# A hybrid decoder layer on one core: turned query and key rows split over 128 partitions, and another order of the last products of the output projection

## The chip, the cores and the metric

The kernel runs on one core of a Trainium2 chip. The metric is the device time of one execution in microseconds (us), lower is better. The engines are TensorE (PE in the profile, its weight loads PEld), VectorE (DVE), ScalarE (ACT), GpSimd (POOL) and SyncE (SP), which issues nearly all DMAs. Each engine works through its own list in order; semaphores tie the lists together.

## The reference

One decoder layer over 1024 tokens of width 1024, all in float32. One normed input projection feeds two groups of heads; their outputs are joined, projected, added to the residual and passed through a squared-ReLU MLP.

```python
h = rms_norm(x, norm1_w[l])
proj = h @ w_in[l]
da_q = rms_norm(da_q.reshape(B, S, DA_HEADS, 2, DA_QK_DIM), q_norm_w[l])   # 4 heads, two 64-wide maps each
da_k = rms_norm(da_k.reshape(B, S, DA_HEADS, 2, DA_QK_DIM), k_norm_w[l])
da_o = diff_attention(da_q, da_k, da_v, lam)     # (softmax(q1 k1^T) - lam * softmax(q2 k2^T)) v, causal
...
dn_o = gated_delta_rule(dn_q, dn_k, dn_v, g, beta)      # 4 heads, 128 wide, chunks of 64
...
mix = jnp.concatenate([da_o.reshape(B, S, DA_WIDTH), dn_o.reshape(B, S, DN_WIDTH)], axis=-1)
x = x + mix @ w_out[l]
h = rms_norm(x, norm2_w[l])
x = x + jnp.square(jax.nn.relu(h @ w_up[l])) @ w_down[l]
```

## The kernel before

**Precision.** Products that need more than one pass of the array take each float32 operand as a rounded part (fp32r, names ending in H) and a remainder (names ending in L), and sum three matmuls: high by high, high by low, low by high. Lines 1012 to 1014, 1291 to 1293 and 1452 to 1454 are such triples, each matmul 128x128 by 128x512.

**Tokens** come in 8 blocks of 128 (NT = 8). `tiles` lists them from the last to the first, and the projection's position i means block `tiles[i]`.

**Stages.** Up to about 260 us come the input norm, the projections of the gated DeltaNet heads and the preparation of their chunks. From 260 to about 620 us several streams are woven together. After that the MLP runs as two Strassen-like series of products with nothing else beside it.

**The planner.** The woven stretch is written as Python generators: `scan` and `scan_out` (the DeltaNet recurrence), `da_units` (the projection for the differential attention), `da_turns` (transposes of its normed queries and keys), `scores` and `values` (softmax and its product with v), `mix_loads` and `mixed` (transposes of the heads' outputs), `outproj` (output projection and second norm), `backs` and `up_first` (transposes and the first products of the MLP). `Interleave` holds a clock, `flow.now`, that only TensorE's work advances (`flow.pe`); `flow.chain` books the costs of ACT and DVE steps and gives the time when a result should be there. At each step the generator of the lowest priority number that is due goes on. So TensorE's order is fixed by these estimates when the kernel is built; the other engines' instructions and the DMAs are ordered by the framework's own scheduling. A put-off store (`flow.put_off`) is issued when its planned time is reached, or before its buffer is taken again (`flow.begun`).

**Queries and keys.** `da_units` makes for each token block 512 projected columns; `leave` (from line 1027) copies them out on ACT (lines 1035 and 1040), norms them per 64 columns and hands tiles of 256 columns (two heads) to `late`. For each of 32 such tiles (two pairs of heads, query or key, 8 blocks) `da_turns` does two transposes (lines 965 and 966) into one bank of `px`, a PSUM pool with two banks that five other streams use too. The bank then holds 128 partitions, 64 for each of the two softmax maps of a head, by two heads of 128 tokens. For map m the rounded rows go to their own 64 partitions of `qa[:, m]` and the remainder to the other 64, so that one contraction over 128 partitions gives high by high plus low by low, and with the halves swapped (`qb`) the two cross terms. That is two ACT instructions (line 972) and two DVE ones (line 973) over 64 partitions each. One DMA (line 977) stores the 256 KB tile to `qk_d`; `qa` has two buffers. `load_head` (line 1068) reads the keys of a head back as `KS`, `load_q` (lines 1085 to 1087) the queries of a block as `qa` and `qb`, both in pieces of 512 bytes.

**Weights.** `load_unit` brings a unit's weights through two buffers `wraw` (line 211), rounds them on ACT (line 213) and takes the remainder on DVE (line 214). The last such units here are those of the output projection.

**Output projection.** `outproj` first adds the products of the DeltaNet half of `mix`. Then `todo` holds 16 products of the attention half, each 12 matmuls for one block and one half of the columns (n = 0 left, n = 1 right): all left ones first, then all right ones. It takes the first in the list whose block has landed; a right one needs its left one done, and either all scores done and i < 4, or `state["free"]`, which `mixed` sets after the last block has been turned. Each product is added to `accs` (line 1298). After the right one `norm2` stores the row of 1024 (line 1308, 512 KB), squares it on ACT (line 1310) and scales it on DVE (line 1316) into `hn`, a tile of the pool `ae` that has four buffers and otherwise holds the softmax tiles `pexp`. `backs` turns the normed blocks: those of i < 4 through `keep`, which takes a row tile of the eight that `accs` used (lines 250 to 257), the others through `turn_b` (line 1384). `feed` fills further row tiles with the first weights of the MLP (line 1430).

Of the kernel before, what the change touches and what calls it, by code (L numbers as in the profile page):

```python
# [9 lines left out]
F32 = mybir.dt.float32  # L10
F32R = mybir.dt.float32r
BF16 = mybir.dt.bfloat16
AF = mybir.ActivationFunctionType
ALU = mybir.AluOpType
# [4 lines left out]
P = 128  # L19
# [3 lines left out]
NT = SEQ // P  # L23
# [96 lines left out]
def act(n, accum=False):  # L120
    return "S", 55.0 + 0.83 * n + (93.0 if accum else 0.0)


def vec(n, extra=0.0):
    return "V", 68.0 + 1.045 * n + extra
# [7 lines left out]
def tile_hymba_layer(  # L133
# [6 lines left out]
    nc = tc.nc  # L140
    V, S, G, T = nc.vector, nc.scalar, nc.gpsimd, nc.tensor
# [9 lines left out]
    dram = ctx.enter_context(tc.tile_pool(name="dram", bufs=1, space=DRAM))  # L151
# [36 lines left out]
    fsg_d = dram.tile([P, 1024], F32, name="fsg_d")  # L188
    rt_d = dram.tile([SEQ], F32, name="rt_d")
    cgr_d = dram.tile([HEADS * SEQ], F32, name="cgr_d")  # L190
    qk_d = dram.tile([2, 2, NT, P, 2, 2, P], F32, name="qk_d")
    v_d = dram.tile([NT, P, 3, P], F32, name="v_d")
    acc_d = dram.tile([NT, P, DM], F32, name="acc_d")
    ud = {i: dram.tile([FF // 512, P, 2, 512], F32, name=f"ud{i}") for i in range(1, 8)}
# [261 lines left out]
    for tb in range(NT):  # L456
        T.matmul(tail[:, 300 + 2 * tb:302 + 2 * tb], ssum_[:, tb * P:(tb + 1) * P], ones[:, 0:2],
                 start=True, stop=True)
# [288 lines left out]
    ae = actx.enter_context(tc.tile_pool(name="ae", bufs=4, **right))  # L747
# [16 lines left out]
    flow = Interleave()  # L764
# [189 lines left out]

    late, accs, vts, v_at, qa_free = [], {}, {}, {}, [0.0] * 3

    def da_turns():
        for i in range(4 * NT):
            while not late:
                yield flow.now + 50, None  # L960
            g, kind, tb, qn, t = late[0]
            r = yield from flow.bank("px", at=max(t + 2000, qa_free[i % 2] - 500))
            late.pop(0)
            pt = px.tile([P, 512], F32, tag="px", name="ps_qkt")
            T.transpose(pt[:, 0:P], qn[:, 0:P], ident)
            T.transpose(pt[:, P:2 * P], qn[:, P:2 * P], ident)
            flow.begun(("qa", i % 2))
            qa = sd.tile([P, 2, 256], F32R, tag="qa", name="qa", bufs=2)
            wv = qw if kind == 0 else kw
            for m in range(2):  # L970
                a, b = HF[m], HF[1 - m]
                S.activation(qa[a, m, :], pt[a, 0:256], AF.Copy, scale=wv[a])
                V.scalar_tensor_tensor(qa[b, m, :], pt[a, 0:256], wv[a], qa[a, m, :].bitcast(F32),
                                       ALU.mult, ALU.subtract)
            flow.pe(2 * TR)
            t = flow.chain(act(256), act(256), vec(256, 60), vec(256, 60), start=max(flow.now, qa_free[i % 2]))
            flow.put_off(t, ("qa", i % 2), lambda g=g, kind=kind, tb=tb, qa=qa: nc.sync.dma_start(
                qk_d[g, kind, tb], qa.bitcast(F32).rearrange("p m (h t) -> p m h t", h=2)))
            qa_free[i % 2] = t + DMA_T
            flow.hold(r, t)  # L980
            state["turned"] += 1
            if state["turned"] % (2 * NT) == 0:
                flow.due(lambda t, key: key[0] == "qa")
                state["da"] += 1
                state["da_t"] = flow.now + 6000
        sdctx.close()
# [77 lines left out]
    def load_head(h, pool):  # L1064
        KS = []
        for m in range(2):
            k = pool.tile([P, SEQ], F32R, tag=f"KS{m}", name=f"KS{m}")
            nc.sync.dma_start(k.bitcast(F32).rearrange("p (b t) -> p b t", t=P),
                              qk_d[h // 2, 1, :, :, m, h % 2, :].rearrange("b p t -> p b t"))
            KS.append(k)  # L1070
        return KS

# [8 lines left out]
    def load_q(h, tb):  # L1081
        qa = ap.tile([P, 2, P], F32R, tag="qa", name="qa", bufs=2)
        qb = ap.tile([P, 2, P], F32R, tag="qb", name="qb", bufs=2)
        src = qk_d[h // 2, 0, tb, :, :, h % 2, :]
        nc.sync.dma_start(qa.bitcast(F32), src)
        nc.sync.dma_start(qb[HF[0]].bitcast(F32), src[HF[1]])
        nc.sync.dma_start(qb[HF[1]].bitcast(F32), src[HF[0]])
        return qa, qb

    order = [(0, t) for t in range(NT)] + [(1, t) for t in range(NT)]  # L1090
    order += [(h, t) for t in reversed(range(NT)) for h in (2, 3)]
    ready = []

    def scores():
        heads, loaded, npe, nsc, since = {}, {}, 0, 0, 0
# [5 lines left out]
        for u, (h, tb) in enumerate(order):  # L1101
# [29 lines left out]
            n = (tb + 1) * P  # L1131
            npc = 1 if n <= 512 else 2
            pl = n // npc
            pe, ssum = [], ap.tile([P, 2], F32, tag="ssum", name="ssum", bufs=4)
            mx = ap.tile([P, 2], F32, tag="mx", name="mx", bufs=4)
            for m in range(2):
                nsc += 1
                if state["scan"] and nsc % 2:
                    name, sc = "rsc", pools["rsc"]
                else:  # L1140
                    name, sc = "qsc", qsc
                yield 0, name
                sc = sc.tile([P, 1024], F32, tag="sc", name="ps_sc")
                for pc in range(npc):
                    o = sc[:, 512 * pc:512 * pc + pl]
                    ks = KS[m][:, pc * pl:(pc + 1) * pl]
                    last = pc == npc - 1
                    T.matmul(o, qa[:, m, :], ks, start=True, stop=False)
                    T.matmul(o, qb[:, m, :], ks, start=False, stop=not last)
                    if last:  # L1150
                        T.matmul(sc[:, 512 * pc + pl - P:512 * pc + pl], identr, caus, start=False, stop=True)  # L1151
                scv = sc.rearrange("p (a b) -> p a b", b=512)[:, :npc, :pl]
                V.tensor_reduce(mx[:, m:m + 1], scv, axis=AX.XY, op=ALU.max, negate=True)  # L1153
                npe += 1
                ep = pools["be"] if state["scan"] and npe % 3 == 0 else ae
                e = ep.tile([P, SEQ], F32, tag="pexp", name="pexp")
                S.activation(e[:, :n].rearrange("p (a b) -> p a b", a=npc), scv, AF.Exp, bias=mx[:, m:m + 1],  # L1157
                             accum_out=ssum[:, m:m + 1])
                flow.pe(2 * max(n / 2.4, 110.0) + 55)
                t = flow.chain(vec(n), act(n, True))  # L1160
                flow.hold(name, t)
                pe.append(e)
# [4 lines left out]
            V.scalar_tensor_tensor(pe[0][:, :n], pe[1][:, :n], cf, pe[0][:, :n], ALU.mult, ALU.add)  # L1167
            t = flow.chain(vec(10), vec(1, 60), vec(n, 100), start=t - flow.HOP)
            q = load_q(*order[u + 1]) if u + 1 < len(order) and order[u + 1][0] // 2 < state["da"] else None
            ready.append((h, tb, pe[0], ri, vt, t))  # L1170
        state["scored"] = True

    turn_no = [0]
# [1 line left out]
    def values():  # L1175
        for _ in order:
            while not ready or ready[0][5] > flow.now:
                yield (flow.now + 100 if not ready else ready[0][5]), None
            h, tb, pe, ri, vt, _t = ready[0]
            while v_at.get(tb, 1e12) > flow.now:  # L1180
                yield flow.now + 50, None
            vt = vt or vts[0]
# [96 lines left out]
    def outproj():  # L1279
# [23 lines left out]
        def norm2(tb, pos):  # L1303
            w2b = pools["w2b"] if state["free"] else w2b0
            hn = ae.tile([P, SEQ], F32, tag="pexp", name="hn2")
            hn = [hn[:, 0:512], hn[:, 512:1024]]
            ss = laid("nss")
            nc.sync.dma_start(acc_d[tb], accs[tb])
            for i in range(2):
                S.activation(hn[i], accs[tb][:, 512 * i:512 * i + 512], AF.Square, accum_out=ss[:, i:i + 1])  # L1310
            V.tensor_tensor(ss[:, 0:1], ss[:, 0:1], ss[:, 1:2], ALU.add)
            r = laid("nr")
            rstd(r, ss[:, 0:1], 1.0 / DM, EPS, None, "nrt", 1)
            for i in range(2):
                sl = slice(512 * i, 512 * i + 512)
                normed_by[:] = [V.scalar_tensor_tensor(hn[i], accs[tb][:, sl], r, w2b[:, sl], ALU.mult, ALU.mult)]
            t = flow.chain(act(512, True), act(512, True), vec(1), vec(1), ("G", 1800.0))
            return hn, flow.chain(vec(512, 60), vec(512, 60), start=t - flow.HOP)
# [17 lines left out]
        aw = dctx.enter_context(tc.tile_pool(name="aw", bufs=1, **right))  # L1336
        w2b0 = aw.tile([P, DM], F32, name="w2b0")
        nc.sync.dma_start(w2b0, norm2_w.partition_broadcast(P))
        todo = [(n, i) for n in range(2) for i in range(NT)]
        left0 = NT  # L1340
        flow.add(6, up_first())
        flow.add(4.5, backs())
        while todo:
            j = next((j for j, (n, i) in enumerate(todo) if landed.get((tiles[i], 0), 1e12) <= flow.now
                      and (n == 0 or (0, i) not in todo) and (n == 0 or state["scored"] and i < 4 or state["free"])), None)
            if j is None:
                yield flow.now + 50, None
                continue
            n, i = todo.pop(j)
            yield from half(0, (w0, w1)[n], n, tiles[i])  # L1350
            if n == 0:
                left0 -= 1
                if left0 == 0:
                    pools["wu"] = first_ops(0), unit_time("V", 610.0)
            else:
                hns[i] = norm2(tiles[i], i)
                normed2.add(i)
                feed()
# [496 lines left out]
```

## Time and profile before

| | us |
|---|---|
| time before, median of 3 runs (1225.75 to 1227.22) | 1226.64 |
| the profiled execution | 1226.58 |
| its span, first to last instruction | 1224.9 |
| ACT at line 972, 64 instructions | 29.26 |
| DVE at line 973, 64 instructions | 30.48 |
| TensorE's waits of 0.2 us and more, summed | 9.1 |

The stretches and their busy time tell where an engine sits idle; a wait is named by the line that waited and by what ended it. Matmuls overlap, so their durations add up to more than the time that they take, and the distance between two starts is what counts. The granted clock is 1.00 nearly everywhere.

### The profile page before, as it was taken

To read this page: it belongs to the slowest core of one execution; us is meant where nothing else is said; L and a number is where in the kernel's file an instruction comes from. 1 tells how busy PE (TensorE), PEld (TensorE's weight loads), DVE (VectorE), ACT (ScalarE), POOL (GpSimd) and SP (SyncE) were. 2 spreads that over 40 slices of the span, in tenths; PEclk is the share of its full clock that TensorE was granted. 3 is DMA by queue.
4 is the path that set the end of the run, shared out by engine and by line. 5 is a ranking of instruction groups with operands and counts; after the bars stand their busy time and mean duration, and the time that the engine had idled before them with its cause. 6 is when DMAs were issued, how large, how long until landed. Compare 5 with 4: busy or idle time off the path is not lost.

```text
span 1224.9 us, 17632 instructions
## 1 busy us (share of the span) xinstructions
PE 1212.0 (99%) x6330; PEld 1029.2 (84%) x6330; DVE 850.0 (69%) x1448; ACT 604.6 (49%) x1176; POOL 121.0 (10%) x162
## 2 busy tenths in 40 slices
PE   9999999999999999999999999999999999999998
PEld 9988888898888888888788888888888888888887
DVE  7786788477868577766798554566577955786553
ACT  8565545234556555656666444454554333333331
POOL 0011110223332230212100000000000000000000
PEclk9999999999999999999999999999999999999999
DMA  6564442456755584434528433443279855433301
GB/s 230 176 182 125 112 130 87 116 183 218 241 161 180 173 244 135 115 80 142 183 86 291 155 127 133 170 174 135 103 253 353 325 185 183 160 104 104 138 35 69
DMA packets 161087, 199.04 MB, mean 163 GB/s; under 512 B 21008, under 2 KB 120936, under 8 KB 161000
## 3 DMA queue, kind: packets, MB, share of 16 engines
q1 hardware_dynamic: 160856, 197.79, 49.3%
q8 instruction: 50, 0.82, 0.3%
q14 instruction: 37, 0.30, 0.1%
q10 hardware_dynamic: 144, 0.13, 0.0%
HBM read 132.32 MB, written 65.56 MB: 162 GB/s over the span
## 4 chain that ended last, share of the span: by engine, by line
PE 89%; DVE 4%; DMA 3%; ACT 2%; issue 1%; SPq 0%; POOL 0%; ACTq 0%; DVEq 0%
PE X L1454 5%; PE X L1453 5%; PE X L1452 5%; PE X L1768 4%; PE X L1769 4%; PE X L1770 4%; PE ps_dn L221 4%; PE ps_dn L219 4%; PE ps_dn L220 4%; PE ps_qk L1012 3%; PE Y L1454 3%; PE Y L1453 3%; PE Y L1452 3%; PE ps_qk L1014 3%; PE ps_qk L1013 2%; PE ps_o L1201 2%
## 5 line engine op out<-in xcount | busy, mean ns | idle before, releaser
L1371 ACT CAST hH<-ur 128x1024 fp32r<-128x1024 f32 x56 | 58.6, 1048 | 166.0 <-PE X L1769 79.7
L1372 DVE TENSOR_TENSOR hL<-ur,hH 128x1024 fp32r<-128x1024 f32 x56 | 68.5, 1224 | 79.8 <-ACT hH L1371 79.8
L1372 DVE TENSOR_TENSOR op<-raw,op 128x1024 fp32r<-128x1024 f32 x48 | 58.7, 1223 | 75.3 <-PE X L1453 42.3
L1768 PE MATMUL X<-hH 128*128 128x512 f32 x224 | 87.2, 389 | 0.0
L1769 PE MATMUL X<-hL,hH 128*128 128x512 f32 x224 | 87.2, 389 | 0.0
L1770 PE MATMUL X<-hH,hL 128*128 128x512 f32 x224 | 87.2, 389 | 0.0
L1012 PE MATMUL ps_qk<-wH,hH 128*128 128x512 f32 x192 | 82.2, 428 | 1.9 <-ACT qn L1040 1.9
L1014 PE MATMUL ps_qk<-wH,hL 128*128 128x512 f32 x192 | 75.8, 395 | 0.0
L219 PE MATMUL ps_dn<-hH,wH 128*128 128x512 f32 x192 | 75.7, 394 | 0.0
L220 PE MATMUL ps_dn<-hL,wH 128*128 128x512 f32 x192 | 75.6, 394 | 0.0
L1013 PE MATMUL ps_qk<-wL,hH 128*128 128x512 f32 x192 | 75.4, 393 | 0.1
L221 PE MATMUL ps_dn<-hH,wL 128*128 128x512 f32 x192 | 75.4, 393 | 0.0
L1372 DVE TENSOR_TENSOR hL<-dw,hH 128x1024 fp32r<-128x1024 f32 x56 | 68.2, 1220 | 3.2 <-ACT hH L1371 3.2
L1371 ACT CAST op<-raw 128x1024 fp32r<-128x1024 f32 x48 | 50.4, 1050 | 34.8 <-PE Y L1454 20.1
L1371 ACT CAST hH<-dw 128x1024 fp32r<-128x1024 f32 x56 | 58.6, 1047 | 16.7 <-DMA dw<-in_w_down_dram 5.1
L1157 ACT ACTIVATE pexp<-ps_sc,mx 128x128 f32<-128x128 f32 (+7 forms) x64 | 47.3, 740 | 26.1 <-DVE mx L1153 26.1
L595 DVE SCALAR_TENSOR_TENSOR cy<-cp,pv,cy 128x512 f32<-128x512 f32 x72 | 53.7, 750 | 7.8 <-ACT cy L593 7.0
L1153 DVE TENSOR_REDUCE mx<-ps_sc 128x1 f32<-128x128 f32 (+7 forms) x64 | 47.5, 754 | 14.1 <-PE ps_sc L1151 13.5
L1291 PE MATMUL ps_op<-wH,hH 128*128 128x512 f32 x128 | 53.6, 419 | 0.0
L1293 PE MATMUL ps_op<-wH,hL 128*128 128x512 f32 x128 | 50.3, 393 | 0.0
L1292 PE MATMUL ps_op<-wL,hH 128*128 128x512 f32 x128 | 50.0, 391 | 0.0
L1453 PE MATMUL Y<-hL,op 128*128 128x512 f32 x128 | 49.8, 389 | 0.0
(355 smaller groups left out, 3383.8 us busy)
## 6 DMA issues: line engine op xcount, KB each, us to landing
ur<-ud SPq DMA_DIRECT2D x28, 1024.0 KB, 4.9
raw<-in_w_up_dram SPq DMA_DIRECT2D x32, 512.0 KB, 3.7
dw<-in_w_down_dram SPq DMA_DIRECT2D x32, 512.0 KB, 7.2
qk_d<-qa SPq DMA_DIRECT2D x32, 256.0 KB, 3.1
ud<-ua SPq DMA_DIRECT2D x16, 512.0 KB, 4.0
ud<-s SPq DMA_DIRECT2D x16, 512.0 KB, 3.2
wraw<-in_w_in_dram SPq DMA_DIRECT2D x24, 256.0 KB, 3.5
wraw<-in_w_in_dram SPq DMA_DIRECT2D x48, 128.0 KB, 2.9
```

Source lines behind the costliest of these rows:

```text
L219: T.matmul(ps, lh(k), rh(k), start=(k == 0), stop=False)
L220: T.matmul(ps, lh(k), rl(k), start=False, stop=False)
L221: T.matmul(ps, ll(k), rh(k), start=False, stop=(k == n - 1))
L1012: T.matmul(ps, hH[:, 4 * kh + k, sl], wh[:, k, :], start=(kh + k == 0), stop=False)
L1013: T.matmul(ps, hH[:, 4 * kh + k, sl], wl[:, k, :], start=False, stop=False)
L1014: T.matmul(ps, hL[:, 4 * kh + k, sl], wh[:, k, :], start=False, stop=(kh + k == 4))
L1371: S.copy(dst[0], src)
L1372: V.tensor_tensor(dst[1], src, dst[0].bitcast(F32), ALU.subtract)
L1453: T.matmul(ps, op[0][:, k, cs], h[1][:, k, :], start=False, stop=False, skip_group_check=True)
L1768: T.matmul(o, v[0][:, j, sl], v[2][:, j, c], start=s0, stop=False, skip_group_check=True)
L1769: T.matmul(o, v[0][:, j, sl], v[3][:, j, c], start=False, stop=False, skip_group_check=True)
L1770: T.matmul(o, v[1][:, j, sl], v[2][:, j, c], start=False, stop=s1, skip_group_check=True)
```

## The change

The names of the diff are those of the section before. The turned tile is split once: ACT rounds all 128 partitions into `qa[:, 0]`, DVE writes the remainder of all 128 into `qa[:, 1]`. Since `qk_d` shall still hold, for each map, 64 high and 64 low rows (for the second map low first), its index is now map, row, head, token, and `store_halves` writes each tile with two DMAs of 128 KB: the rounded rows to the first and fourth block of 64 rows, the remainder to the second and third. The planner books one ACT and one DVE step instead of two and two. The loads read the same 512-byte pieces under the new index.

In `outproj`, `todo` lists left and right products of positions 0 to 3, then those of 4 to 7. `in_ae` counts the tiles taken from `ae`; each entry of `ready` carries the number of its first softmax tile, and before `free` a right product may only run if the next tile of `ae` doesn't take the place of one that an entry of `ready` still holds.

```diff
-    qk_d = dram.tile([2, 2, NT, P, 2, 2, P], F32, name="qk_d")
+    qk_d = dram.tile([2, 2, NT, 2, P, 2, P], F32, name="qk_d")
...
+    def store_halves(dst, qa):
+        blocks = dst.rearrange("m (j r) h t -> (m j) r (h t)", j=2)
+        for part, to in ((0, blocks[0:4:3]), (1, blocks[1:3])):
+            nc.sync.dma_start(to, qa[:, part, :].bitcast(F32))
...
-            for m in range(2):
-                a, b = HF[m], HF[1 - m]
-                S.activation(qa[a, m, :], pt[a, 0:256], AF.Copy, scale=wv[a])
-                V.scalar_tensor_tensor(qa[b, m, :], pt[a, 0:256], wv[a], qa[a, m, :].bitcast(F32),
-                                       ALU.mult, ALU.subtract)
+            S.activation(qa[:, 0, :], pt[:, 0:256], AF.Copy, scale=wv)
+            V.scalar_tensor_tensor(qa[:, 1, :], pt[:, 0:256], wv, qa[:, 0, :].bitcast(F32), ALU.mult, ALU.subtract)
             flow.pe(2 * TR)
-            t = flow.chain(act(256), act(256), vec(256, 60), vec(256, 60), start=max(flow.now, qa_free[i % 2]))
-            flow.put_off(t, ("qa", i % 2), lambda g=g, kind=kind, tb=tb, qa=qa: nc.sync.dma_start(
-                qk_d[g, kind, tb], qa.bitcast(F32).rearrange("p m (h t) -> p m h t", h=2)))
+            t = flow.chain(act(256), vec(256, 60), start=max(flow.now, qa_free[i % 2]))
+            flow.put_off(t, ("qa", i % 2), lambda g=g, kind=kind, tb=tb, qa=qa: store_halves(qk_d[g, kind, tb], qa))
...
-                              qk_d[h // 2, 1, :, :, m, h % 2, :].rearrange("b p t -> p b t"))
+                              qk_d[h // 2, 1, :, m, :, h % 2, :].rearrange("b p t -> p b t"))
...
-        src = qk_d[h // 2, 0, tb, :, :, h % 2, :]
+        src = qk_d[h // 2, 0, tb, :, :, h % 2, :].rearrange("m p t -> p m t")
...
+                mine.append(in_ae[0] if ep is ae else 1e9)
+                in_ae[0] += ep is ae
...
-            ready.append((h, tb, pe[0], ri, vt, t))
+            ready.append((h, tb, pe[0], ri, vt, t, mine[0]))
...
-        todo = [(n, i) for n in range(2) for i in range(NT)]
+        todo = [(n, i) for g in range(2) for n in range(2) for i in range(4 * g, 4 * g + 4)]
...
-                      and (n == 0 or (0, i) not in todo) and (n == 0 or state["scored"] and i < 4 or state["free"])), None)
+                      and (n == 0 or (0, i) not in todo) and (n == 0 or state["free"] or state["scored"] and i < 4 and all(in_ae[0] - 4 < x[6] for x in ready))), None)
```

More of the change, by code (lines that the diff above doesn't have):

```diff
@@ L1091, in tile_hymba_layer @@
     order += [(h, t) for t in reversed(range(NT)) for h in (2, 3)]
-    ready = []
+    ready, in_ae = [], [0]
     def scores():
@@ L1133, in scores @@
             pl = n // npc
+            mine = []
             pe, ssum = [], ap.tile([P, 2], F32, tag="ssum", name="ssum", bufs=4)
@@ L1178, in values @@
                 yield (flow.now + 100 if not ready else ready[0][5]), None
-            h, tb, pe, ri, vt, _t = ready[0]
+            h, tb, pe, ri, vt, _t, _ = ready[0]
             while v_at.get(tb, 1e12) > flow.now:
@@ L1305, in norm2 @@
             hn = ae.tile([P, SEQ], F32, tag="pexp", name="hn2")
+            in_ae[0] += 1
             hn = [hn[:, 0:512], hn[:, 512:1024]]
```

## The prediction

> **What bounds the kernel now.** I read the page's spans, then TensorE's waits, then busy time and granted clock by stretch, then the chain of waits behind the largest gap, then the DMA view of single stores.
>
> ```profile
> span 1224.9 us, 17632 instructions
> PE 1212.0 (99%) x6330; PEld 1029.2 (84%) x6330; DVE 850.0 (69%) x1448; ACT 604.6 (49%) x1176; POOL 121.0 (10%) x162
> ```
>
> TensorE is busy for 1212.0 of 1224.9 us. The change removes no matmul, so the question is what it does to the 12.9 us of gaps, to the clock, and whether it opens new gaps. Four rows of TensorE's timeline show that order alone costs nothing:
>
> ```profile
> 532.51 0.60 PE L1189 MATMUL ps_at<-ident,pexp 128*128 128x128 f32 x4
> 532.86 0.48 PE L1291 MATMUL ps_op<-wH,hH 128*128 128x512 f32 x1
> 533.18 0.40 PE L1292 MATMUL ps_op<-wL,hH 128*128 128x512 f32 x1
> 533.41 0.39 PE L1293 MATMUL ps_op<-wH,hL 128*128 128x512 f32 x1
> ```
>
> Starts count, not durations: in steady state a 512-column matmul follows every 0.23 us. Four small ones and the first large one take 0.67 us together, so a small one costs 0.11 us wherever it stands. A new order of the same matmuls moves the time only through waits.
>
> ```profile
> 258.00:620.00 362.00, 354.48 (x2065) 305.90 (x2066) 266.88 (x629) 208.55 (x544) 88.67 (x109) 1.00 0.57 174
> 306.40:308.80 2.40, 0.49 (x4) 0.07 (x2) 2.31 (x5) 1.71 (x5) 0.51 (x1) 1.00 0.89 248
> 308.80:313.00 4.20, 4.20 (x17) 3.78 (x18) 4.07 (x9) 3.05 (x10) 2.54 (x3) 0.60 0.54 179
> 345.00:350.00 5.00, 5.00 (x27) 4.14 (x26) 3.77 (x13) 3.92 (x16) 3.39 (x4) 1.00 0.31 95
> ```
>
> Columns: stretch, length, busy us of PE, PEld, DVE, ACT, POOL, then granted clock, DMA share and GB/s. In the whole region that the change touches TensorE idles 362.00 - 354.48 = 7.5 us. The gap before 308.80 is followed by 4.2 us at clock 0.60, a further loss of 4.2 x 0.40 = 1.7 us.
>
> ```profile
> PE ps_qk L1012 <- ACT qn L1040: 1.9, 1, 1.9
> ```
>
> ```profile
> 342.68 0.33 PE L1189 MATMUL ps_at<-ident,pexp 128*128 128x128 f32 x1 [0.95 <-DVE pexp L1167]
> ```
>
> This longest wait is the 306.4 gap; with its slow clock it costs 3.6 us. The 0.95 us gap before 342.68 left the clock at 1.00 (the row 345 to 350). The Trainium skill, page "TensorE: Matmul & The Clock Gate", section "Part 1: The HAM clock gate", has the clock halve after at least one idle window of about 3.4 us; here 1.9 us were enough, so the measurement decides (by the rule the gap would be worth 1.9 us, not 3.6).
>
> **Part 1, the splits.** Before, each of the 32 turned tiles takes two ACT and two DVE instructions over 64 partitions; after, one each over 128.
>
> ```profile
> L972 ACT ACTIVATE qa<-ps_qkt,pv x32: 456/469/472, 261.5 to 393.9; 64x256 fp32r<-64x256 f32 x32
> ...
> L973 DVE SCALAR_TENSOR_TENSOR qa<-ps_qkt,pv,qa x32: 476/482/490, 262.5 to 395.7; 64x256 fp32r<-64x256 f32 x32
> ```
>
> ```profile
> 559.09 0.47 ACT L1157 ACTIVATE pexp<-ps_sc,mx 128x256 f32<-128x256 f32 x1
> 560.81 0.48 DVE L1167 SCALAR_TENSOR_TENSOR pexp<-pexp,cf 128x256 f32<-128x256 f32 x1
> ```
>
> The same operations at 128x256 take 0.47 and 0.48 us, so half of the work goes: 32 x 0.47 = 15 us of ACT and 32 x 0.48 = 15 us of DVE. Neither engine is the bound; the removal counts only where they end a wait.
>
> ```profile
> by line: DMA wraw<-in_w_in_dram 22.1%; DVE qa L973 12.7%; issue 12.2%; ACT osq L919 9.1%; DVE oc L914 6.1%; DVE S L881 4.9%; ACT qa L972 4.2%; DVE oc L924 4.0%; DVE sn L1052 3.2%; ACT qn L1040 3.0%; DVE sy L866 3.0%; DVE wL L214 2.8%; ACT w
> ...
> 299.45 5.06 DMA wraw<-in_w_in_dram
> ...
> 308.05 0.70 ACT qn L1040
> ```
>
> This is the chain from 286.5 to 309.4 (22.9 us) behind the gap. DVE's and ACT's splits hold 16.9% of it, 3.9 us, so halving them takes 1.9 us out, as much as the gap. In between stands a weight load of 5.06 us. So part 1 would be worth up to 3.6 us, **if its stores do no harm**.
>
> **Part 1, the stores.** One store of 256 KB becomes two of 128 KB. SP issues 32 more:
>
> ```profile
> L977 SPq DMA_DIRECT2D qk_d<-qa x32: 319/327/778, 264.6 to 455.7; - x32
> ```
>
> ```profile
> qk_d<-qa SPq DMA_DIRECT2D x32, 256.0 KB, 3.1
> ...
> v_d<-qn SPq DMA_DIRECT2D x8, 128.0 KB, 1.7
> ```
>
> That is 32 x 0.33 = 10.5 us of SP over 191 us; before a weight load it can cost 0.33 us. Key and query loads then wait for two landings. A 128 KB store lands in 1.7 us, so two spread ones cost no more than one of 3.1. But are they spread? The rounded halves go to two blocks of 64 rows that lie three blocks apart, the remainders to two adjacent blocks. How a store is dealt out shows in two that run alone, a 4 KB one of 8 rows and a 64 KB one of 128 rows (the 17th packet of the first, over 8 KB, is not the store's):
>
> ```profile
> DMA packets 17, 0.02 MB, mean 13 GB/s; under 512 B 8, under 2 KB 16, under 8 KB 16
> ...
> rt_d<-rts SPq DMA_DIRECT2D x1, 4.0 KB
> ```
>
> ```profile
> DMA packets 144, 0.07 MB, mean 39 GB/s; under 512 B 16, under 2 KB 144, under 8 KB 144
> ...
> mixa_d<-om SPq DMA_DIRECT2D x1, 64.0 KB, 1.6
> ```
>
> 128 rows close with 16 short end packets; the 8 rows of 512 B are followed by 8: the queue deals a DMA out by its outer count. If the rounded half is carried as 2 outer blocks of 64 rows, it lies on **two of the 16 DMA engines**, 64 KB on each. The adjacent blocks can run together as 128 rows.
>
> ```profile
> 300.00:305.00 5.00, 5.00 (x34) 4.43 (x33) 1.79 (x6) 1.03 (x2) 0.61 (x1) 1.00 0.87 306
> ```
>
> ```profile
> q1 hardware_dynamic: 13003, 14.29, 73.4%
> ...
> qk_d<-qa SPq DMA_DIRECT2D x13, 256.0 KB, 3.4
> ```
>
> The first row gives an engine's pace (DMA share 0.87, 306 GB/s): 306 / (0.87 x 16) = 22 GB/s, so 64 KB take 3.0 us, against 16 KB or 0.74 us per engine for the whole store before. The other two are the stretch 275 to 337 with 13 stores. There each engine works 0.734 x 62 = 45.5 us, 9.6 of it for these stores. On the two engines it becomes 45.5 - 9.6 + 13 x (3.0 + 0.37) = 79.7 us in 62: **17.7 us too much**. Every other load has a sixteenth on each of them and lands with them. What is queued behind is all that SP issues: weights (L211), the scan's chunks (L839, L894), queries; TensorE's order is fixed, so it waits. Some of the delay is covered: the 5.06 us load left a gap of 1.9 us, so about 3.2 us of flight are hidden. Price: 17.7 - 3.2 = 14.5 us. Bounds: below, a spread store, -3.6; above, both stores on two engines, 45.5 - 9.6 + 13 x 6.0 = 113.9, or 52 us too much in this stretch alone. I take 14.5, since the 8-row store is the nearest row and the destination has its step of two outermost.
>
> The rule stands in the Trainium skill, page "DMA: Bandwidth & Descriptors", section "Why a DMA increments its semaphore by 16 and not by 1": the engine count is the largest up to 16 that divides the slowest dimension of both sides. By it two blocks give two engines; the 8-row store agrees, and no run here shows a store of two blocks.
>
> **Part 2, the order.** Every product, store and norm stays; the right-half products of blocks 0 to 3 now stand before the left halves of 4 to 7. The fourth of them moves forward past up to three left halves (12 matmuls of 0.23 us each, 8 us in all), and with it one 512 KB store, two ACT squares and two DVE scalings. The guard keeps a norm from taking a buffer that waiting scores hold; while products are left over, TensorE is covered.
>
> ```profile
> PE ps_tr L1384 <- DVE hL L257: 1.1, 1, 1.1
> ```
>
> ```profile
> 601.44 4.53 DMA acc_d<-acc
> 606.04 0.59 ACT kept L254
> 607.14 0.70 DVE hL L257
> ```
>
> The 1.1 us gap lies just before 608 and ends this chain: a kept tile waits for an accumulator's store issued at 601.44. With the fourth block's norm done earlier, this should go: -1.1 us. Bounds: -1.1 (no wait is left there) to +3.4 (a kept tile late by a whole store of 4.5 us, less the 1.1).
>
> **Sum**, against the profiled execution (span 1224.9, whole 1226.58, 0.06 below the shown median of 1226.64): +14.5 for the stores, in which the 306 gap is absorbed, -1.1 for the order: 1226.6 + 13.4 = **1240.0 us**.
>
> **Rivals.**
> - *Spread stores, faster.* If the store's rows are dealt out over all 16 engines, the 306 gap closes with its slow clock (-3.6), the 608 gap goes (-1.1), and one gap like the 0.95 us one opens, since the order is laid anew: 1222.8. It decides at a landing of about 3 us; for it speaks only that I have not seen a two-block store.
> - *A wash.* Stores spread, but a weight load is late elsewhere and another gap with a slow clock opens: -4.7 + 3.6 = 1225.5; or the two engines' queue drains in lulls such as 345 to 350 (share 0.31).
> - *Both stores on two engines*, if the remainders keep the two blocks too: 52 - 3.2 - 1.1, about 1274 or more.
> - *The change does not do what it says*: an operation over 128 partitions taking twice as long would leave the engines' loads alone. The 0.47 and 0.48 us rows speak against it; the time would be that of the stores.
>
> **Chances.** Rounded half on two engines, slower: 0.52. Both on two: 0.07. Spread and faster: 0.25. A wash: 0.16. A measurement of this kernel tells about 0.2%, 2.5 us, from no change. So faster 0.25, same 0.16, slower 0.59. The forecast's own range is 1231 to 1254: half of the overload hidden, or 17.7 us with clock losses of 1.7 us after several gaps. To hold 8 in 10 the range must reach the faster case: 1221 to 1256.
>
> **What would show it.** Right: qk_d stores land in 5 us or more, weight and park_d loads between 270 and 400 take longer, ACT and DVE wait on DMA, TensorE's busy share between 258 and 460 falls, its clock dips; L972 and L973 stand at 32 instructions of 0.47 and 0.48 us. Wrong: stores land in 2 us and the 306 gap is gone, then the store was spread. For part 2: no wait on acc_d before the first L1384. If 600 to 620 holds a longer gap, the guard or the store order cost more than I gave it.

## The result, and the profile after

| | before | after |
|---|---|---|
| median of 5 runs, us | 1226.74 (1225.75 to 1227.22) | 1262.9 (1261.72 to 1267.01) |
| after / before, 95% interval | | 1.0303 [1.0283, 1.0324] |
| profiled execution: span, us | 1224.9 | 1261.2 |
| granted clock, mean | 0.998 | 0.989 |

The change costs 36.2 us; the forecast was 13.4, and its range ended at 1256.0. The first lines of the page of after, the span and the busy times:

```profile
span 1261.2 us, 17634 instructions
...
PE 1225.3 (97%) x6330; PEld 1038.6 (82%) x6330; DVE 828.0 (66%) x1416; ACT 589.8 (47%) x1144; POOL 122.3 (10%) x162
```

ACT and DVE do less, as the change says. TensorE does the same 6330 matmuls. It idles 1261.2 - 1225.3 = 35.9 us instead of 12.9, which is 23.0 us, and is busy for 13.3 us longer: 36.3 us together, the difference of the two spans. The lower mean clock accounts for most of the second part, (0.998 - 0.989) x 1261.2 = 11.4 us. Where this happens shows in the busy times by stretch (length, busy us of PE, PEld, DVE, ACT, POOL, clock, DMA share, GB/s), first of before, then of after:

```profile
275.00:337.00 62.00, 60.07 (x361) 52.54 (x359) 51.75 (x136) 29.77 (x79) 20.24 (x21) 0.97 0.74 232
345.00:400.00 55.00, 54.85 (x296) 46.23 (x295) 40.90 (x99) 35.38 (x92) 15.40 (x21) 1.00 0.58 176
400.00:460.00 60.00, 58.62 (x324) 50.22 (x322) 39.25 (x96) 34.39 (x85) 18.90 (x23) 1.00 0.70 210
460.00:560.00 100.00, 98.70 (x611) 87.46 (x610) 71.08 (x144) 57.48 (x147) 17.73 (x22) 1.00 0.39 113
```

```profile
275.00:337.00 62.00, 53.49 (x293) 44.93 (x293) 38.42 (x107) 18.96 (x54) 18.57 (x19) 0.94 0.67 189
345.00:400.00 55.00, 47.94 (x263) 41.10 (x263) 32.49 (x90) 27.31 (x80) 11.66 (x15) 0.94 0.57 159
400.00:460.00 60.00, 54.93 (x293) 46.52 (x292) 28.77 (x83) 26.69 (x75) 17.06 (x21) 0.97 0.58 162
460.00:560.00 100.00, 95.68 (x561) 83.95 (x560) 68.11 (x127) 56.16 (x126) 21.20 (x24) 0.97 0.52 156
```

The loss is not in one place. TensorE's idle time grows by 6.6, 6.9, 3.7 and 3.0 us in the four stretches, and in each the clock is 0.03 to 0.06 lower. The DMA share falls in the first stretch although more DMAs are to be moved: the queues as a whole are not full. The stores, the splits and who waited for the stores, from the view of one tile (its DMAs' issue times in ns, min, median and max, with the first and last start, then the waits in us and times):

```profile
L960 SPq DMA_DIRECT2D qk_d<-qa x64: 382/500/2283, 262.7 to 487.3; - x64
...
who waited for it (us, times):
  ACT qa L975: 27.6, 7
  PE ps_sc L1150: 8.2, 3
  PEld ps_sc L1150: 6.4, 1
  DVE qa L976: 5.9, 3
```

```profile
L975 ACT ACTIVATE qa<-ps_qkt,pv x16: 453/473/477, 261.9 to 418.6; 128x256 fp32r<-128x256 f32 x16
...
L976 DVE SCALAR_TENSOR_TENSOR qa<-ps_qkt,pv,qa x16: 472/482/485, 262.7 to 419.7; 128x256 fp32r<-128x256 f32 x16
```

The turn stage, from first to last store, takes 487.3 - 262.7 = 224.6 us; before it took 455.7 - 264.6 = 191.1. The splits do what they should (two such groups of 16 on each engine, at 0.47 and 0.48 us), but ACT now waits 27.6 us for the stores, where it waited once before, for 2.8 us:

```profile
  ACT qa L972: 2.8, 1
```

The chain of waits shows how long the stores that were waited for are under way (start, length, what):

```profile
264.52 7.13 DMA qk_d<-qa
...
273.79 7.46 DMA qk_d<-qa
...
286.04 7.34 DMA qk_d<-qa
```

Before, the same 256 KB landed in 3.1 us in one DMA, in the median of all 32; the view gives no such median for after. TensorE's longest waits after, by what ended them (us in total, times, longest):

```profile
PE ps_sc L1150 <- DMA KS<-qk_d: 6.2, 1, 6.2
PE ps_qk L1013 <- ACT qn L1041: 3.5, 1, 3.5
PE ps_sc L1150 <- ACT pexp L1161: 3.2, 2, 2.7
PE ps_tr L1389 <- ACT hn L1390: 2.4, 1, 2.4
```

The page counts the DMA packets of before and after by size:

```profile
DMA packets 161087, 199.04 MB, mean 163 GB/s; under 512 B 21008, under 2 KB 120936, under 8 KB 161000
```

```profile
DMA packets 165248, 199.05 MB, mean 158 GB/s; under 512 B 21072, under 2 KB 129192, under 8 KB 165160
```

The packets under 512 B hold the short end packets, one for each DMA engine that a DMA uses. Before, 32 stores closed with 16 each, 512. After there are 64 more: 576 = 32 x 16 + 32 x 2. So one of the two stores of a tile lies on 16 engines and the other on **two**, as the forecast inferred from a store of 8 rows. The Trainium skill, page "DMA: Bandwidth & Descriptors", section "Why a DMA increments its semaphore by 16 and not by 1", states the rule: the number of engines is the largest up to 16 that divides the slowest dimension of both sides. The two end packets of each store here agree with it. The page adds that such a DMA, issued from SP, takes the lowest-numbered engines, so by it all 32 stores would meet on the same two. The trace doesn't name the engines, but the pace of such stores in a row (e12 below) shows that they share two.

### The profile page after: what moved, and what is told of

Its sections match the earlier page's. It is cut to its first block, busy times and chain, and to the rows that moved or that the text cites. A ratio compares the mean times of both kernels' runs of the same rounds, so it can differ in the third digit from the quotient of the medians.

```text
span 1261.2 us, 17634 instructions
## 1 busy us (share of the span) xinstructions
PE 1225.3 (97%) x6330; PEld 1038.6 (82%) x6330; DVE 828.0 (66%) x1416; ACT 589.8 (47%) x1144; POOL 122.3 (10%) x162
## 4 chain that ended last, share of the span: by engine, by line
PE 84%; DMA 9%; ACT 2%; issue 2%; DVE 1%; SPq 1%; POOL 1%; ACTq 0%; DVEq 0%; POOLq 0%
PE X L1459 5%; PE X L1457 5%; PE X L1458 5%; PE X L1774 4%; PE X L1773 4%; PE X L1775 4%; DMA qk_d<-qa 4%; PE ps_dn L219 3%; PE ps_dn L221 3%; PE ps_dn L220 3%; PE Y L1459 2%; PE Y L1457 2%; PE Y L1458 2%; PE ps_qk L1013 2%; PE Z L1774 2%; PE Z L1773 2%
## 5 line engine op out<-in xcount | busy, mean ns | idle before, releaser
L213 ACT CAST wH<-wraw 128x512 fp32r<-128x512 f32 x64 | 37.2, 625 | 36.6 <-DMA wraw<-in_w_in_dram 22.7
```

## Experiments

"Before" ran beside every experiment on the same chip, between 1226.1 and 1226.8 us.

| kernel | us (median) | to before, 95% interval |
|---|---|---|
| after | 1262.9 | 1.0303 [1.0283, 1.0324] |
| e1, stores by partition half (16 engines) | 1230.48 | 1.0035 [1.0023, 1.0047] |
| e2, splits and stores alone | 1261.51 | 1.0288 [1.0274, 1.0301] |
| e3, order alone | 1226.03 | 1.0001 [0.9992, 1.0010] |
| e4, both stores on two engines | 1322.19 | 1.0782 [1.0763, 1.0801] |
| e5, before with two spread stores | 1230.08 | 1.0034 [1.0022, 1.0046] |
| e6, new splits, one store, more loads | 1232.22 | 1.0054 [1.0041, 1.0067] |
| e9, e1 with the order of before | 1228.39 | 1.0022 [1.0012, 1.0031] |
| e8, every second tile as after | 1239.74 | 1.0118 [1.0104, 1.0132] |
| e10, two-block store issued by ACT | 1273.6 | 1.0394 [1.0372, 1.0415] |
| e11, e9 with half of the stores issued by ACT | 1228.13 | 1.0013 [1.0004, 1.0022] |
| e12, extra stores, issued early | 1297.72 | 1.0585 [1.0567, 1.0602] |
| e13, extra two-block stores in place | 1280.27 | 1.0445 [1.0427, 1.0464] |
| e14, extra spread stores in place | 1239.59 | 1.0109 [1.0094, 1.0124] |

### Only the dealing out (e1)

```diff
-        for part, to in ((0, blocks[0:4:3]), (1, blocks[1:3])):
-            nc.sync.dma_start(to, qa[:, part, :].bitcast(F32))
+        for m in range(2):
+            nc.sync.dma_start(blocks[2 * m:2 * m + 2].rearrange("s r f -> r s f"), qa[HF[m]].bitcast(F32))
```

For the second map the high rows now come first; the queries and the keys change alike, so the products are the same.

> The kernel after, with its two stores of a tile cut by partition halves instead of by rounded and remainder: each store takes 64 partitions with both rows of 1 KB, so its outermost step is 64 rows and not 2 blocks. Same bytes, same 64 stores, same 1 KB rows, same splits, same order. Theory A (the two-block store lies on two DMA engines, and all loads land with these): the loss goes, 1222 to 1228 us, landings back to some 2 to 3 us, no ACT qa wait on DMA. Rival B (twice the stores, or 1 KB rows instead of 2 KB, are the cost): stays at 1258 to 1265. Rival C (the new order of the products): stays as well, less only the DMA waits of ACT.

1230.48 us. Same bytes, same 64 stores, same 1 KB rows, same splits and order: the dealing out is worth 1262.9 - 1230.5 = 32.4 of the 36.2 us. (It also changes which rows share a store; e13 and e14 below change the target addresses alone.) Rivals B and C fall. ACT's wait for the stores goes back to 2.2 us, and the stores land in 2.8 us in the median:

```profile
  ACT qa L975: 2.2, 2
```

The page of e1 has 512 more packets under 512 B than before, 64 x 16 end packets for 32 x 16:

```profile
DMA packets 165696, 199.05 MB, mean 162 GB/s; under 512 B 21520, under 2 KB 129640, under 8 KB 165608
```

But 4.3 us above before remain, and the time is 2.5 us above the expected range, where the forecast's rival of spread stores had a gain.

### Each part alone (e2, e3)

e2 puts back `todo = [(n, i) for n in range(2) for i in range(NT)]` and the guard of before in the kernel after; e3 puts the new list and the new guard in the kernel before.

> The kernel after, with the order of the output projection's products and its guard put back to those of before; splits and stores stay. Theory A: all the loss stays, 1260 to 1265 us (the 1.1 us gap before the first norm back, the 2.4 us gap of after gone). Rival C (the order costs): under 1250.

> The kernel before, with only the order of the products and its guard from the change. Theory A: 1224 to 1228 us, my step of -1.1 or nothing. Rival C: 1235 or more.

1261.51 and 1226.03 us: the stores and splits carry the loss, and the order alone is 1.0001 [0.9992, 1.0010], nothing. The forecast's gap before 608 stays in e3 (TensorE's timeline: start, length, instruction, idle time before it and what ended that):

```profile
607.85 0.63 PE L1388 MATMUL ps_tr<-ident,hn 128*128 128x128 f32 x4 [0.89 <-DVE hL L257]
```

1.12 us became 0.89, not 0. In e1, with the new order, another gap of 2.31 us stands at the same step and waits for ACT:

```profile
620.33 0.65 PE L1389 MATMUL ps_tr<-ident,hn 128*128 128x128 f32 x4 [2.31 <-ACT hn L1390]
```

### The dose (e4, e8)

e4 stores the remainders as two distant blocks too:

```diff
-        for part, to in ((0, blocks[0:4:3]), (1, blocks[1:3])):
-            nc.sync.dma_start(to, qa[:, part, :].bitcast(F32))
+        for part in range(2):
+            nc.sync.dma_start(blocks[part:4:2], qa[:, part, :].bitcast(F32))
```

> The kernel after, with the remainders also stored as two blocks of 64 rows that lie two blocks apart (rounded rows to blocks 0 and 2, remainders to 1 and 3): both stores of a tile are now two-block stores, bytes and counts unchanged. Theory A: the two engines get twice the load of after; from +36 us at 3.0 us a tile to about +80 to +100 at 6.0 us a tile, 1305 to 1330 us, and 64 more end packets fewer than with spread stores. Rival B and C: no change, 1258 to 1266.

e8 stores tiles with odd `i` as e1 and tiles with even `i` as after.

> The kernel after, with every second turned tile stored by partition half: 16 two-block stores instead of 32, everything else as in after. Theory A1 (capacity: the slowdown sets in when the two engines' own work fills the turn stage, some 103 to 115 us of other work plus 16 x 3.4 plus 16 x 0.7, about 170 to 180 of 192 us: it still fits): 1231 to 1239. Theory A2 (each two-block store costs its own delay, whatever the load): half of the step from 1230.5 to 1262.9, 1244 to 1249.

With 0, 16, 32 and 64 two-block stores the times are 1230.5, 1239.7, 1262.9 and 1322.2 us: the first 16 cost 9.3, the next 16 cost 23.2, the next 32 cost 59.3. That is neither a fixed price for each store (A2: 1244 to 1249 for 16) nor free up to a threshold; e8 lies just above A1's range. What bends the curve shows when the work of the two engines is set against the stage's length. The queue's share of the 16 engines in the turn stage of after (262.7 to 487.3 us) and then of e4 (261.8 to 544.4 us), the columns packets, MB, share:

```profile
q1 hardware_dynamic: 43906, 39.14, 61.7%
```

```profile
q1 hardware_dynamic: 43558, 39.24, 46.0%
```

The share times the length is the mean work of an engine. A two-block store adds to it, on each of the two, 64 KB in place of its mean part of 8 KB. With 2.71 us for 64 KB (e12 below), that is 2.71 x 7/8 = 2.37 us a store:

| kernel | stage, us | mean work of an engine | work of the two, worked out | share of the stage |
|---|---|---|---|---|
| before | 191.1 | 66.4% = 126.9 | 126.9 | 66% |
| e1 | 193.9 | 71.2% = 138.1 | 138.1 | 71% |
| e8 | 204.5 | 68.6% = 140.3 | 140.3 + 16 x 2.37 = 178.2 | 87% |
| after | 224.6 | 61.7% = 138.6 | 138.6 + 32 x 2.37 = 214.4 | 95% |
| e4 | 282.6 | 46.0% = 130.0 | 130.0 + 64 x 2.37 = 281.7 | 100% |

By this working, in e4 two engines are busy for the whole stage and set its length; the mean of 46% hides them. In after they are nearly there. At 87% the stage is already 10.6 us longer than in e1; part of that is the run, since the profiled execution of e8 was its slowest (1242.6 us) and that of e1 one of its fastest (1228.8). The last two columns are worked out, since the trace doesn't say which engine moved a packet, and are good to about a tenth (e12 below says why); the end packets of e4 (32 x 16 - 64 x 2 = 384 fewer than before) say that all its stores use two:

```profile
DMA packets 164800, 199.05 MB, mean 151 GB/s; under 512 B 20624, under 2 KB 128744, under 8 KB 164712
```

### Engine or queue (e10)

The two-block store is issued by ACT, `(nc.sync if part else nc.scalar).dma_start(...)`.

> The kernel after, with the rounded (two-block) store issued by ACT instead of SP; the remainders' store stays with SP. The two engines carry as much as in after, but SP's loads no longer stand behind these stores in SP's own queue. Theory A1 (the two engines' capacity): 1252 to 1270, little changed. Theory F (loads stand behind the stores in the order of one queue): 1245 or less.

1273.6 us, above the range of A1 and 10.7 slower than after. Theory F falls: SP's loads don't stand behind these stores in SP's queue alone, and another queue doesn't help here. The Trainium skill, page "DMA: Bandwidth & Descriptors", section "Issuing engines are not separate DMA queues", states that DMAs of all issuing engines run on the same 16 DMA engines and interleave. The 1273.6 us agree with it. Why it is slower yet isn't settled: ACT now issues 32 DMAs of 0.50 us, 16 us, and waits for stores for 35.0 us instead of 27.6.

### Through all loads, or through those that wait for the store (e12, e13, e14)

e12 takes e1 and adds to each tile one 128 KB two-block store, of a tile that isn't rewritten, to a scratch that nothing reads.

```diff
+        nc.sync.dma_start(ex_d[i, 0:4:3], hH[:, 7, 0:256].bitcast(F32))
```

> The stores by partition half as in the first run (1230.5), and beside them one extra 128 KB two-block store a tile, from a tile that is not rewritten in this stage to a scratch that nothing reads: the two engines carry about what they carry in after (64 KB more a tile), but no ring buffer and no key or query load waits for these stores. Theory A1 (capacity, through all other loads): 1255 to 1270. Theory G (the two-buffer ring of turned tiles and the key loads that wait for the slow stores are the cost): 1232 to 1242.

1297.72 us, and it answers another question: since these stores wait for nothing, they were issued at 25.1 to 125.7 us, in a stage before the turns. The timeline of SP there, and the group of the extra stores:

```profile
28.07 27.12 SPq L962 DMA_DIRECT2D ex_d<-hH  x10
```

```profile
L962 SPq DMA_DIRECT2D ex_d<-hH x32: 478/2568/5700, 25.1 to 125.7; - x32
```

Ten issues in 27.12 us: 2.71 us for 64 KB on an engine, 24 GB/s, near the forecast's 3.0. From 28 to 55 us these stores are all that the queue moves (packets, MB, share of the 16 engines):

```profile
q1 hardware_dynamic: 1290, 1.30, 13.6%
...
ex_d<-hH SPq DMA_DIRECT2D x11, 128.0 KB
```

13.6% of 16 engines is 2.2 engines, where two full ones would be 12.5%. So the store is on two engines here too, and stores in a row are on the same two: on different pairs they would run side by side and the share would be higher. The excess over 12.5% is most simply read as packet times that overlap by about a tenth; the shares in the table above are sums of such times, which limits what 95% and 100% there can mean.

The median issue takes 2.57 us, where the same instruction in e13 takes 0.53. SP itself is held up, and with it the weight loads it has still to issue; the turn stage begins at 331.6 us instead of 262.9. e13 holds each extra store back until its tile's two stores are issued, and e14 does the same with adjacent blocks, `ex_d[i, 1:3]`:

```diff
+        with tc.issue_after(st.ins):
+            nc.sync.dma_start(ex_d[i, 0:4:3], hH[:, 7, 0:256].bitcast(F32))
```

> The extra two-block stores of the run before were issued far ahead of the turned tiles, from 25 to 126 us, so they measured another stage. Here each is held back until its tile's two stores have been issued. Nothing waits for it: no ring buffer and no key or query load. The two engines carry about what they carry in after. Theory A1 (capacity, through all other loads and SP's own queue): 1255 to 1275. Theory G (the two-buffer ring of turned tiles and the key loads that wait for the slow stores): 1236 to 1245.

> The control for that run: the same extra 128 KB a tile, in the same place, to two adjacent blocks, so that it is spread over the engines. It prices 32 more issues and 4 MB more: 1231 to 1236 by either theory; the difference between the two runs is the dealing out alone.

1280.27 and 1239.59 us, both above their ranges: 32 more spread stores cost 9.1 us over e1, and that the same bytes lie on two engines costs 40.7 us more, though nothing waits for these stores. Theory G falls: the loss comes without any wait for a two-block store. What such waits add in after isn't shown. ACT's longest wait for a DMA in e13:

```profile
ACT qa L978 <- DMA qk_d<-qa: 31.2, 8, 6.2
```

ACT waits 31.2 us for stores of e13 that are themselves spread over 16 engines. In e14 it is 5.3 us, with 7.0 us more before the same line that are put down to a load of `pka`. A sixteenth of each lies behind the extra store on the two engines, and the whole store lands with it. This is the forecast's mechanism apart from any wait for the two-block stores themselves. The two engines' work in e13, worked out as above, is 62.7% of 241.3 + 75.8 = 227.1 us, 94% of its stage.

### What the spread stores leave (e5, e6, e9, e11)

e5 is the kernel before with the new scratch layout and a store for each column half of the old tile (`nc.sync.dma_start(dst[m]..., qa[:, m, :]...)`); splits and order stay. e6 has the new splits and one 256 KB store of 128 rows of 2 KB, and cuts the loads by halves instead. e9 is e1 with the order of before; e11 is e9 with one of the two stores issued by ACT.

> The kernel before, with the scratch layout of after and one 128 KB store for each column half m of the old tile: 128 rows of 1 KB, spread, 64 stores instead of 32; the four split instructions and the order stay. By the stores by partition half (1230.5) a rest of +4.4 us is open. Theory D (twice the stores, with twice SP's issue time, are that rest): 1228 to 1232. Theory E (the rest is a new place of waits, from the new splits' shorter chain or from the order): 1225 to 1228.

> The splits over 128 partitions as in after, but one 256 KB store a tile as before (128 rows of 2 KB), the order of before, and loads cut by halves instead (a query tile 4 loads of 64 KB instead of 3, a key tile 2 of 256 KB instead of 1). Theory D: the splits alone are free or a small gain, 1222 to 1227, if 40 more loads cost nothing. Theory E: 1228 to 1232. My step of up to -3.6 us for the splits is right only at 1224 or less.

> The stores by partition half and the new splits, with the products' order of before. Tells whether the order costs the 2.3 us gap before the first left-over norm (1.1 us before): then 1228 to 1229.5; if it costs nothing, 1230 to 1232.

> The stores by partition half with the order of before (1228.4), with the lower half's store of each tile issued by ACT instead of SP. Theory D1 (the doubled stores cost SP's time: 64 of 0.6 us instead of 32 of 0.33): 1225 to 1227.5. Theory D2 (their landings, twice as many DMAs, are the cost): 1228 to 1230. If ACT's issue time is what counts: over 1230.

1230.08, 1232.22, 1228.39 and 1228.13 us. e5: to store the tile in two DMAs, with the loads under the new index, costs 3.7 us, so theory D's size is right. e6: to save them with 40 more loads costs more, 5.8. e9 against e5: with the new splits it is 1.7 us less, but the runs of the two overlap (1226.59 to 1231.63 and 1227.58 to 1231.89) and the form of the stores differs as well, so it is no more than a hint. e9 against e1: the new order may cost 2.1 us beside the new stores (2.3 us of gap); the intervals overlap. After against e2, the same step, is 1.4 us, with intervals that overlap too. e11: no gain that can be told from e9, so it isn't shown that SP's issue time is the price of the second store.

No version is shown to beat the kernel before.

## Why the prediction was right or wrong

1. **What bounds the kernel; order costs nothing by itself.** Right: e3 is 1.0001.

2. **The splits, up to -3.6 us.** The instructions came out as forecast, 32 of 0.47 and 32 of 0.48 us. The gap at 306 did close where the stores do no harm; e1's row of that stretch:

```profile
275.00:337.00 62.00, 60.23 (x363) 52.33 (x362) 44.97 (x128) 26.17 (x77) 20.01 (x21) 1.00 0.82 237
```

Its clock is 1.00 instead of 0.97. But TensorE idles 1.8 us there against 1.9 before: three shorter gaps, the longest of 1.2 us behind ACT's rounding of a weight, stand in place of the one. The largest gap of e1's turn stage is this one, which before doesn't have:

```profile
393.47 1.80 PE L1205 MATMUL ps_o<-vt,at 128*128 128x128 f32 x14 [2.04 <-DVE qa L976]
```

So the removal was measured at 1.7 us (e9 against e5), which isn't certain.

3. **Two spread stores cost no more than one.** Wrong by 3.7 us (e5). The step compared landings, 1.7 with 3.1 us, and priced SP's 10.5 us of more issues at nothing. The issues are also longer than the 0.33 us of the row used: 0.38 us for 128 rows of 1 KB (e5), 0.60 for 64 rows of two pieces (e1). Which of issue and landing it is stays open (e11).

4. **The rounded half on two engines, +14.5 us.** The mechanism was right in the links that the trace shows: two end packets, landings of over 5 us (7.1 to 7.5 on the chain), ACT and DVE waiting on DMA, TensorE's share falling between 258 and 460, its clock lower. That the weight loads took longer shows only in ACT's wait for them, 22.7 us against 14.1 (18.4 in e1). The size was not right: e1 puts it at 32.4 us. **The term that was mis-sized is the overload, 17.7 - 3.2 us.** It was summed over one stretch of 62 us with 13 of the 32 stores, as if the rest of the stage could work it off. The same arithmetic over the whole stage of before, 126.9 + 32 x (3.0 + 0.37 - 0.74) = 211.1 us of work in 191.1, gives 20.0 too much, and the measured stage is 33.5 us longer. So the choice of the stretch explains 2.3 us of the miss and no more. What is left has two parts, one read from the trace and one worked out: the mean work of an engine grew from 126.9 to 138.6 us for the same bytes (138.1 with spread stores, where 71% hides it), and the two engines may not be full all the time (95%, by the pace of e12, good to about a tenth); loads and stores stand in a fixed order, and TensorE's own waits, such as the 6.2 us for `KS`, put off what comes next. How the 33.5 us divide among these isn't shown. The 3.2 us of cover did not show as such.

5. **The clock.** The forecast's sum had no term for it; "clock losses of 1.7 us after several gaps" stood only in its range. TensorE's busy time is 13.3 us longer, 11.4 of them by the mean clock, about a third of the whole loss. The waits alone, 23.0 us, would have come to about 1250. So of the 22.9 us by which the sum fell short, 9.6 are waits (23.0 against 13.4) and 13.3 are TensorE's longer busy time, which the sum put at nothing though its own reading had priced the slow clock behind one gap at 1.7 us.

6. **The order, -1.1 us.** Wrong in size: e3's interval is -1.0 to +1.2 us. The gap before the first turned block of the second norm stays.

7. **The rivals.** "Spread stores, faster" gave 1222.8 us for a spread store; e1, which is that case, took 1230.5, so it fails at points 2, 3 and 6. Of the forecast's times, the 1225.5 of "a wash" comes nearest to e1; that after took 1262.9 says that its backlog did not drain in lulls. "Both stores on two engines" was put at 1274 or more; e4 took 1322.2.

## What to carry to other kernels

Before a store is rearranged, look at the outermost step of its target: 2 blocks there, with 128 partitions on the other side, put 128 KB on two of 16 DMA engines. Such stores took 7 us where they were waited for, in place of 3, and held up DMAs that were spread (31.2 us of waits in e13), while the mean DMA share went down. Price such a hot spot over the whole stage that shares these engines, not over the busiest stretch, and add a term for the slow clock behind the gaps that it opens in TensorE (here 11.4 us beside 23.0 us of waits). Two DMAs for one are not free even when they are spread: 32 more cost 3.7 us here, and 32 more with 4 MB more, which nothing waits for, 9.1.

## What the runs showed of the hardware that was not expected

- An issue on SP is no fixed cost. With two engines backed up it took 2.57 us in the median (e12), up to 5.70, and all that SP had still to issue waited. Reading it as a full queue is an inference; the row shows the pace of the two engines.
- The median issue time of a store went from 0.33 to 0.60 us: 0.33 for 128 rows of 2 KB (before; the same form took 0.38 in e6), 0.38 for 128 of 1 KB (e5), 0.50 for two blocks of 64 rows from ACT (e10), 0.60 for 64 rows of two pieces (e1). The form is not all of it: two adjacent blocks took 0.39 in e10 and 0.59, from another tile, in e14.
- The mean work of an engine for about the same bytes differs with the stores: 126.9 us in the stage before, 138.1 in e1. Packets of 1 KB in place of 2 KB don't explain it, since e5 has as many of them as e1 and worked 130.2 us (67.0% of 194.3). What does is open.
